# Two layers of a hybrid decoder trunk: the forget gates' chain goes first in both layers, and the final norm's steps stand in another order

## The chip, the cores and the metric

The kernel runs on one core of one Trainium2 chip. The core has a matrix engine (TensorE, PE in the profile; its weight loads are PEld), three engines for elementwise work (VectorE is DVE, ScalarE is ACT, GpSimd is POOL) and SyncE (SP), which here issues nearly all DMA transfers. Each engine works through its own list of instructions in order; semaphores hold an instruction until what it needs is there. TensorE writes to PSUM, of which the kernel uses eight banks. The metric is the device time of one execution in microseconds.

## The reference: what is computed

528 positions (16 learned meta tokens and 512 real ones) of width 1024 pass through two layers. Each layer is

```
xn   = rmsnorm(h) ; proj = xn @ w_in        # q,k,v of 8 fox heads, 8 gate columns, q,k,v,g of 4 retention heads
logf = log_sigmoid(gate columns + bias) ; c = cumsum(logf over positions)
fox  = softmax(q.k/8 + c[t] - c[s], causal) @ v           # per head
ret  = silu(g) * groupnorm(decayed linear attention)      # per head
h    = h + concat(fox, ret) @ w_out
h    = h + (silu(hn @ w_gate) * (hn @ w_up)) @ w_down     # hn = rmsnorm(h)
```

and after both layers `rmsnorm(h)` without the meta tokens is returned. Everything is float32.

## The kernel before, in words

Activations lie transposed: the 1024 features of `h` are eight tiles of 128 partitions, the positions run along the free axis. A float32 product is made of three faster ones: each operand is split into a rounded part and a rest (`hi`, `lo`; `split`, L130 to L132, and `convert`), and `hi*hi`, `hi*lo` and `lo*hi` add up in one PSUM bank. ScalarE makes `hi` (whi, xh, ah, sqh), VectorE or, for some weights, GpSimd makes `lo`.

The order of the work. TensorE's list is written out by hand: `layer` builds a plan of steps, and `merge` and `spread` place attention steps between the dense products. The lists of the other engines are made by a planner at build time. It replays the program with its own estimates of times, and gives each engine, whenever it is free, the ready instruction that stands first in the program; instructions under `tc.high_priority()` come ahead of those that don't. An instruction under `pin` is fixed behind the one that was written before it on its engine. The planner also orders SyncE's transfers, and on the chip a transfer whose buffer isn't free holds up all that stand behind it on SyncE.

Weights come as blocks of 512 KB (raw, L147) into three buffers. A buffer is free again when `whi` and `wlo` have been made from it; those lie in a ring of two, so that a conversion waits in turn until TensorE is done with an older block.

The forget gates (`forget_gates`, `forget_sums`). TensorE multiplies the eight gate columns (L368). ScalarE copies the part of the product on partitions 32 to 39 (L374), VectorE adds it to the rest (L375), for two halves of the positions. Then: times the norm's R (L382), absolute value, exponential and logarithm on ScalarE (L383 to L385), the minimum with 0 (L386), a subtraction (L387), and a running sum along the positions (L388). The sums go to a piece of DRAM, `cdr` (L390), and come back per head as `bc`, one row on all partitions (L486, two buffers). The scores of the first head (L497) are PSUM products; VectorE masks them (L503) and combines them with `bc` (L504), and only this frees their bank. PSUM banks `psa` are handed out in turn, four of them, so a later transpose of values (L407) may wait until such a bank is read. In layer 0 all steps up to the logarithm have precedence, in layer 1 none. Around them VectorE also makes q and k from their products (L420 and L427, L433 and L441), ropes (cr and sr, L1258) and value parts (L447).

The end. In the last layer the last round of the down projection is done in two column blocks: A (272 positions) and B (240). Eight products each; after each one VectorE adds it to `h` (`add_part`, L1093). Block A's norm is computed while TensorE is at block B: the steps `after_0` to `after_7` are written between B's products, one behind each. `square_b` and `scale_b` are ScalarE's square of a block of `h` and its product with the norm's weights, `sum_b` (L1131) adds a square to `acc`, `sums` (L1159) adds over partitions on TensorE with a matrix of ones, `root` (L1147) is ScalarE's reciprocal root, `newton` (L1151 to L1155) are three VectorE steps that refine it, and `out_a` and `out_b` multiply two output tiles by the root (L1135) and send them to DRAM (L1138). B's sum of squares is made from five parts: `acc` of squares 0 to 4, split into `hi` and `lo` (L1209, L1210), and squares 5, 6 and 7 as they are. All B steps on VectorE and ScalarE are pinned; the one `out_a` on GpSimd and the transfers aren't.

Of the kernel before, what the change touches and what calls it, by code (L numbers as in the profile page):

```python
# [10 lines left out]
F32 = mybir.dt.float32  # L11
F32R = mybir.dt.float32r
AF = mybir.ActivationFunctionType
ALU = mybir.AluOpType
# [5 lines left out]
T = SEQ + META  # L20
DEPTH = 2
FH = 8
# [17 lines left out]
def hybrid_kernel(ctx, tc, x_t, w_in, w_fl, w_out, w_gate, w_up, w_down, vecs, b_fg, rope, decay, mask, ident, out_t):  # L40
    nc = tc.nc
# [15 lines left out]
    bfg = const.tile([FH, DEPTH], F32, name="bfg")  # L57
# [190 lines left out]
    def psum_a():  # L248
        return psa.tile([128, 512], F32, name="psa", tag="psa")
# [5 lines left out]
    def tt(name, dt=F32):  # L255
        tag, bufs = tags[name]
        return tmp.tile([128, T], dt, name=name, tag=tag, bufs=bufs)
# [38 lines left out]
    def pin(f, pinned=True):  # L296
        if pinned:
            tc.keep_in_program_order(f)
# [48 lines left out]
    def load_gates(l, st):  # L347
        st["wfr"] = wp.tile([128, NK, FH], F32, name="wfr", tag="wfr", bufs=1)
        nc.sync.dma_start(st["wfr"], w_fl[l])
# [6 lines left out]
    def forget_gates(l, st):  # L356
        if l:
            load_gates(l, st)
            gate_weights(l, st)
        else:  # L360
            for t, src in ((bfg, b_fg), (msk, mask), (idt, ident)):
                nc.sync.dma_start(t, src)
        wf = st["wf"]
        psf = [psum_a() for _ in FULL]
        for i in range(2 * NK):
            k, part = i // 2, i % 2
            for ps, (c0, c1) in zip(psf, FULL):
                nc.tensor.matmul(ps[:, 0:c1 - c0], wf[:, k, :], st["x"][k][part][:, c0:c1],  # L368
                                 start=(i == 0), stop=(i == 2 * NK - 1))
        z = tt("z")[0:FH]  # L370
        z2 = tt("z2")[0:FH]
        for ps, (c0, c1) in zip(psf, FULL):
            with ExitStack() if l else tc.high_priority():
                nc.scalar.copy(z2[:, c0:c1], ps[32:32 + FH, 0:c1 - c0])  # L374
                nc.vector.tensor_add(z[:, c0:c1], ps[0:FH, 0:c1 - c0], z2[:, c0:c1])  # L375
        st["z"] = z

    def forget_sums(l, st):
        z = st["z"]
        z2 = tt("z2")[0:FH]  # L380
        with ExitStack() if l else tc.high_priority():
            nc.vector.scalar_tensor_tensor(z, z, RSC, st["R"][0:FH, :], ALU.mult, ALU.mult)  # L382
            nc.scalar.activation(z2, z, AF.Abs, bias=bfg[:, l:l + 1])  # L383
            nc.scalar.activation(z2, z2, AF.Exp, scale=-1.0)
            nc.scalar.activation(z2, z2, AF.Ln, bias=onec[0:FH])  # L385
        nc.vector.tensor_scalar(z, z, bfg[:, l:l + 1], 0.0, ALU.add, ALU.min)  # L386
        nc.vector.tensor_sub(z, z2, z)  # L387
        nc.vector.tensor_tensor_scan(z2, z, z, 0.0, ALU.add, ALU.max)  # L388
        st["cdr"] = tc.dram_tile([FH, T], F32, name=f"cdr{l}")
        nc.sync.dma_start(st["cdr"], z2)  # L390

    LOGS = "natural_log_exp_and_others"
    ROOTS = "abs_reciprocal_sqrt_and_small"
# [419 lines left out]
    def ffn(l, st, real, last):  # L813
# [269 lines left out]
        else:  # L1083
# [4 lines left out]
            na, nb = PA[1] - PA[0], PB[1] - PB[0]  # L1088
            fin = {}
# [24 lines left out]
            def scale_b(*ms):  # L1114
                for m in ms:
                    pin(nc.scalar.activation(fin["yb"][:, m], h[m][:, cb], AF.Copy, scale=gf[:, m:m + 1]))

            def square_b(m):
                if m == 0:
                    t = fft("S", F32, (128, 6, w), 2)  # L1120
                    fin["one"] = [t[:, i, 0:nb] for i in range(3)]
                    fin["acc"], fin["rb"], fin["tb"] = (t[:, i, 0:nb] for i in range(3, 6))
                    d = fin["acc"]
                elif m < NK - 3:
                    fin["sq", m] = d = tt("sq")[:, 0:nb]
                else:
                    d = fin["one"][m - NK + 3]
                pin(nc.scalar.activation(d, h[m][:, cb], AF.Square))

            def sum_b(m):  # L1130
                pin(nc.vector.tensor_add(fin["acc"], fin["acc"], fin["sq", m]))  # L1131
# [8 lines left out]
            def out_a(eng, k):  # L1140
                out(eng, fin["ya"][k // HB][:, k % HB:k % HB + 2], fin["ra"], k, *PA)

            def out_b(eng, k):
                out(eng, fin["yb"][:, k:k + 2], fin["rb"], k, *PB)
# [4 lines left out]
            def newton(i, r, v, a):  # L1149
                if i == 0:  # L1150
                    pin(nc.vector.tensor_mul(a, r, r))  # L1151
                elif i == 1:
                    pin(nc.vector.scalar_tensor_tensor(a, v, D * EPS, a, ALU.add, ALU.mult))
                else:
                    pin(nc.vector.scalar_tensor_tensor(r, a, 3.0 * D, r, ALU.subtract, ALU.mult))  # L1155

            def sums(v, parts):
                for i, t in enumerate(parts):
                    nc.tensor.matmul(v, ones if t.dtype == F32R else ones.bitcast(F32), t, start=(i == 0), stop=(i == len(parts) - 1))  # L1159
# [23 lines left out]
            def after_2():  # L1183
                fin["va"] = psum_a()[:, 0:na]
                sums(fin["va"], fin["a"][0:2])
                fin["ra"], fin["ta"] = (fft("e", F32, (128, T), 2)[:, 0:na] for _ in range(2))
                root(fin["ra"], fin["va"])
                sum_b(1)
                square_b(2)

            def after_3():
                for i in range(3):
                    newton(i, fin["ra"], fin["va"], fin["ta"])
                sum_b(2)
                square_b(3)
                scale_b(0)
                out_a(nc.gpsimd, 0)

            def after_4():
                sum_b(3)  # L1200
                square_b(4)
                scale_b(1)
                out_a(nc.vector, 2)

            def after_5():
                sum_b(4)
                square_b(5)
                hi, lo = tt("sqh", F32R)[:, 0:nb], tt("sql", F32R)[:, 0:nb]
                pin(nc.scalar.copy(hi, fin["acc"]))  # L1209
                pin(nc.vector.tensor_sub(lo, fin["acc"], hi.bitcast(F32)))  # L1210
                fin["b"] = hi, lo
                scale_b(2)

            def after_6():
# [2 lines left out]
            def after_7():  # L1217
                hi, lo = fin["b"]
                square_b(7)
                v = psum_a()[:, 0:nb]  # L1220
                sums(v, (hi, lo, fin["one"][0], fin["one"][1], fin["one"][2]))
                out_a(nc.vector, 4)
                out_a(nc.vector, 6)
                scale_b(3, 4)
                root(fin["rb"], v)
                scale_b(5, 6, 7)
                for i in range(3):
                    newton(i, fin["rb"], v, fin["tb"])
                for k in range(0, NK, 2):
                    out_b(nc.vector, k)  # L1230
# [193 lines left out]
```

## Time and profile before

| | us |
|---|---|
| median of 3 runs (lowest to highest) | 1272.61 (1271.99 to 1272.77) |
| the profiled execution | 1272.43 |
| its span, first to last instruction | 1270.6 |
| TensorE busy in it | 1253.3 (99%) |
| VectorE, ScalarE, GpSimd busy | 998.6, 687.3, 266.9 |
| granted TensorE clock, mean | 0.999 |

A timeline row has its start in microseconds from the beginning of the span, the busy time, the engine and line, the operation, the tile written and the tiles read with their shapes, and how many instructions the row joins. A bracket gives the idle time of the engine in front of it and whose work ended that. Layer 0 takes the span's first half, layer 1 starts near 644, and the last round of the down projection near 1242. Matmuls are pipelined and their ends are modelled, so the rows of TensorE overlap.

### The profile page before, as it was taken

To read this page: it belongs to the slowest core of one execution; us is meant where nothing else is said; L and a number is where in the kernel's file an instruction comes from. 1 tells how busy PE (TensorE), PEld (TensorE's weight loads), DVE (VectorE), ACT (ScalarE), POOL (GpSimd) and SP (SyncE) were. 2 spreads that over 40 slices of the span, in tenths; PEclk is the share of its full clock that TensorE was granted. 3 is DMA by queue.
4 is the path that set the end of the run, shared out by engine and by line. 5 is a ranking of instruction groups with operands and counts; after the bars stand their busy time and mean duration, and the time that the engine had idled before them with its cause. 6 is when DMAs were issued, how large, how long until landed. Compare 5 with 4: busy or idle time off the path is not lost.

```text
span 1270.6 us, 23600 instructions
## 1 busy us (share of the span) xinstructions
PE 1253.3 (99%) x9263; PEld 1195.1 (94%) x9263; DVE 998.6 (79%) x1852; ACT 687.3 (54%) x1246; POOL 266.9 (21%) x527
## 2 busy tenths in 40 slices
PE   9999999999999999999999999999999999999997
PEld 8899999999999999999998989998789999999996
DVE  8878756779888888887786877567899888888866
ACT  7666545676444444444465665456764444444444
POOL 3455545410000000000025546454100000000000
PEclk9999999999999999999999999999999999999999
DMA  6322222123233333332323232222233333333321
GB/s 217 95 71 89 87 81 83 60 68 129 92 96 100 100 100 100 100 100 84 107 70 117 61 101 83 78 90 67 100 96 121 100 100 100 100 100 100 102 81 67
DMA packets 45680, 120.57 MB, mean 95 GB/s; under 512 B 5360, under 2 KB 12272, under 8 KB 45568
## 3 DMA queue, kind: packets, MB, share of 16 engines
q1 hardware_dynamic: 45136, 118.77, 29.7%
q8 instruction: 73, 1.20, 0.4%
q14 instruction: 39, 0.32, 0.1%
q10 hardware_dynamic: 432, 0.29, 0.1%
HBM read 116.91 MB, written 2.13 MB: 94 GB/s over the span
## 4 chain that ended last, share of the span: by engine, by line
PE 93%; DVE 2%; ACT 2%; DMA 2%; issue 0%; SPq 0%; DVEq 0%; ACTq 0%
PE psd L206 29%; PE psa L900 19%; PE psd L1035 14%; PE psd L900 13%; PE psa L206 5%; PE psa L1035 4%; PE psa L407 2%; PE psa L582 2%; PE psa L497 2%; PE psa L749 1%; PE psa L719 1%; DMA bc<-cdr 1%; DMA h<-x_t 0%; DMA cdr<-z 0%; PE psa L279 0%
## 5 line engine op out<-in xcount | busy, mean ns | idle before, releaser
L183 POOL TENSOR_TENSOR wlo<-raw,whi 128x128 fp32r<-128x128 f32 x504 | 261.4, 554 | 270.0 <-ACT whi L180 250.0
L206 PE MATMUL psd<-xh,whi 128*128 128x264 f32 (+1 forms) x792 | 195.4, 314 | 0.2 <-ACT whi L180 0.2
L206 PE MATMUL psd<-xl,whi 128*128 128x264 f32 (+1 forms) x792 | 186.0, 302 | 0.5 <-DVE xl L309 0.4
L206 PE MATMUL psd<-xh,wlo 128*128 128x264 f32 (+1 forms) x792 | 186.4, 303 | 0.0
L206 PEld LDWEIGHTS psd<-xh,whi 128*128 128x128 f32 x792 | 128.0, 189 | 5.2 <-ACT whi L180 0.9
L206 PEld LDWEIGHTS psd<-xh,wlo 128*128 128x128 f32 x792 | 126.8, 188 | 6.3 <-DVE wlo L183 0.6
L206 PEld LDWEIGHTS psd<-xl,whi 128*128 128x128 f32 x792 | 127.4, 188 | 5.0 <-DVE xl L309 1.2
L180 ACT CAST whi<-raw 128x512 fp32r<-128x512 f32 (+1 forms) x168 | 98.4, 613 | 49.3 <-PE psd L206 36.4
L888 ACT CAST whi<-raw 128x1024 fp32r<-128x1024 f32 (+2 forms) x62 | 54.8, 885 | 51.3 <-PE psd L900 39.9
L888 ACT CAST fwhi<-raw 128x1024 fp32r<-128x1024 f32 (+2 forms) x62 | 55.6, 897 | 47.5 <-PE psd L900 40.0
L1135 POOL TENSOR_TENSOR th<-th,e 128x544 f32<-128x544 f32 x1 | 1.4, 1370 | 359.1 <-DVE e L1155 359.1
L85 POOL MEMSET kl<- 64x528 f32 x2 | 1.1, 534 | 345.4 <-PE psa L900 345.4
L889 DVE TENSOR_TENSOR wlo<-raw,whi 128x1024 fp32r<-128x1024 f32 (+2 forms) x62 | 62.9, 1015 | 12.8 <-ACT whi L888 12.7
L889 DVE TENSOR_TENSOR fwlo<-raw,fwhi 128x1024 fp32r<-128x1024 f32 (+2 forms) x62 | 64.0, 1032 | 10.5 <-ACT fwhi L888 10.1
L900 PE MATMUL psa<-th,whi 128*128 128x264 f32 (+1 forms) x232 | 65.4, 282 | 0.0
L900 PE MATMUL psa<-th,wlo 128*128 128x264 f32 (+1 forms) x232 | 65.4, 282 | 0.0
L900 PE MATMUL psa<-tl,whi 128*128 128x264 f32 (+1 forms) x232 | 65.3, 282 | 0.0
L900 PE MATMUL psa<-th,fwhi 128*128 128x264 f32 (+1 forms) x224 | 63.4, 283 | 0.0
L900 PE MATMUL psa<-tl,fwhi 128*128 128x264 f32 (+1 forms) x224 | 63.3, 283 | 0.0
L900 PE MATMUL psa<-th,fwlo 128*128 128x264 f32 (+1 forms) x224 | 63.3, 282 | 0.0
L517 ACT ACTIVATE pd<-pd,nmax 128x144 f32<-128x144 f32 (+1 forms) x64 | 36.9, 576 | 43.8 <-DVE nmax L504 31.8
L966 ACT COPY e<-psa 128x264 f32<-128x264 f32 (+1 forms) x114 | 42.9, 376 | 28.4 <-PE psa L900 24.1
(343 smaller groups left out, 4053.5 us busy)
## 6 DMA issues: line engine op xcount, KB each, us to landing
raw<-w_in SPq DMA_DIRECT2D x54, 512.0 KB, 3.4
raw<-w_gate SPq DMA_DIRECT2D x44, 512.0 KB, 3.8
fraw<-w_up SPq DMA_DIRECT2D x38, 512.0 KB, 3.5
raw<-w_down SPq DMA_DIRECT2D x64, 256.0 KB, 2.8
raw<-w_out SPq DMA_DIRECT2D x16, 512.0 KB, 3.4
raw<-w_down SPq DMA_DIRECT2D x32, 192.0 KB, 2.5
bc<-cdr SPq DMA_DIRECT2D x16, 264.0 KB, 3.5
raw<-w_up SPq DMA_DIRECT2D x6, 512.0 KB, 3.5
```

The lines of the kernel that those rows point to most:

```text
L180: pin(nc.scalar.copy(hi, job["raw"][:, c0:c1]), pinned)
L183: pin(sub(lo[:, i:i + wide], job["raw"][:, c0 + i:c0 + i + wide], hi[:, i:i + wide].bitcast(F32)), pinned)
L206: nc.tensor.matmul(ps[1][b][:, 0:c1 - c0], w[:, wk, :], x[:, c0:c1], start=(k == 0 and i == 0), stop=(k == n - 1 and i == 2))
L407: nc.tensor.transpose(ps[:, 128 * j:128 * j + 128], src[:, o:o + 128], idt)
L497: nc.tensor.matmul(sc[0:nq, 0:c1 - c0], st["q"][s][:, q0:q0 + nq], kk[:, c0:c1], start=(i == 0), stop=(i == 1))
L517: nc.scalar.activation(pr, pr, AF.Exp, bias=nmax[0:nq], scale=-1.0, accum_out=rsum)
L582: nc.tensor.matmul(po[:, c0:SEQ], v[:, j, :], pp[:, j, META + c0:T], start=(j == 0 and i == 0), stop=(j == 4 and i == 1))
L888: nc.scalar.copy(hi, src)
L889: nc.vector.tensor_sub(lo, src, hi.bitcast(F32))
L900: nc.tensor.matmul(bank()[:, 0:b.shape[-1]], a[:, o + k, :], b, start=(fresh and k == 0 and i == 0), stop=(k == n - 1 and i == 2), skip_gr ...
L966: nc.scalar.copy(self.t["e"][:, i], self.t["x"][:, 0:w])
L1035: nc.tensor.matmul(v[:, 0:c1 - c0], a[:, s * n + k, :], b[:, c0:c1], start=(k == 0 and i == 0), stop=(k == n - 1 and i == 2))
```

## The change

Forget gates: in both layers the whole chain, from the copies of the product to the transfer of the sums to DRAM, is under `tc.high_priority()`; before, this held in layer 0 up to the logarithm. The minimum with 0 is written right behind the absolute value.

The end: the three `newton` steps of block A stand behind `root` (`after_2`) instead of behind product 3's addition; `sum_b(2)` moves from `after_3` to `after_4` and `sum_b(3)` from `after_4` to `after_5`; output pair 0 goes from GpSimd to VectorE and one step later, pair 2 to `after_7`; the `lo` part of B's sum is made behind the last addition instead of behind `hi`, and TensorE adds square 5 between `hi` and `lo`; pair 6 is written behind the root's and the scales' lines.

```diff
-            with ExitStack() if l else tc.high_priority():
+            with tc.high_priority():
                 nc.scalar.copy(z2[:, c0:c1], ps[32:32 + FH, 0:c1 - c0])
                 nc.vector.tensor_add(z[:, c0:c1], ps[0:FH, 0:c1 - c0], z2[:, c0:c1])
...
-        with ExitStack() if l else tc.high_priority():
+        with tc.high_priority():
             nc.vector.scalar_tensor_tensor(z, z, RSC, st["R"][0:FH, :], ALU.mult, ALU.mult)
             nc.scalar.activation(z2, z, AF.Abs, bias=bfg[:, l:l + 1])
+            nc.vector.tensor_scalar(z, z, bfg[:, l:l + 1], 0.0, ALU.add, ALU.min)
             nc.scalar.activation(z2, z2, AF.Exp, scale=-1.0)
             nc.scalar.activation(z2, z2, AF.Ln, bias=onec[0:FH])
-        nc.vector.tensor_scalar(z, z, bfg[:, l:l + 1], 0.0, ALU.add, ALU.min)
-        nc.vector.tensor_sub(z, z2, z)
-        nc.vector.tensor_tensor_scan(z2, z, z, 0.0, ALU.add, ALU.max)
-        st["cdr"] = tc.dram_tile([FH, T], F32, name=f"cdr{l}")
-        nc.sync.dma_start(st["cdr"], z2)
+            nc.vector.tensor_sub(z, z2, z)
+            nc.vector.tensor_tensor_scan(z2, z, z, 0.0, ALU.add, ALU.max)
+            st["cdr"] = tc.dram_tile([FH, T], F32, name=f"cdr{l}")
+            nc.sync.dma_start(st["cdr"], z2)
...
                 square_b(2)
-
-            def after_3():
                 for i in range(3):
                     newton(i, fin["ra"], fin["va"], fin["ta"])
-                sum_b(2)
+
+            def after_3():
                 square_b(3)
                 scale_b(0)
-                out_a(nc.gpsimd, 0)
 
             def after_4():
+                sum_b(2)
+                square_b(4)
+                out_a(nc.vector, 0)
+                scale_b(1)
+
+            def after_5():
                 sum_b(3)
-                square_b(4)
-                scale_b(1)
-                out_a(nc.vector, 2)
-
-            def after_5():
                 sum_b(4)
                 square_b(5)
-                hi, lo = tt("sqh", F32R)[:, 0:nb], tt("sql", F32R)[:, 0:nb]
-                pin(nc.scalar.copy(hi, fin["acc"]))
-                pin(nc.vector.tensor_sub(lo, fin["acc"], hi.bitcast(F32)))
-                fin["b"] = hi, lo
+                fin["b"] = tt("sqh", F32R)[:, 0:nb], tt("sql", F32R)[:, 0:nb]
+                pin(nc.scalar.copy(fin["b"][0], fin["acc"]))
                 scale_b(2)
...
             def after_7():
                 hi, lo = fin["b"]
                 square_b(7)
+                pin(nc.vector.tensor_sub(lo, fin["acc"], hi.bitcast(F32)))
                 v = psum_a()[:, 0:nb]
-                sums(v, (hi, lo, fin["one"][0], fin["one"][1], fin["one"][2]))
+                sums(v, (hi, fin["one"][0], lo, fin["one"][1], fin["one"][2]))
+                out_a(nc.vector, 2)
                 out_a(nc.vector, 4)
-                out_a(nc.vector, 6)
                 scale_b(3, 4)
                 root(fin["rb"], v)
                 scale_b(5, 6, 7)
+                out_a(nc.vector, 6)
```

## The prediction

> **What bounds the kernel now.** I read the page first, then the TensorE rows of the timeline wherever the list of TensorE's waits names one, then each stall backwards through the other engines' timelines. The page's first row, and the five TensorE rows with an idle time that the change can reach (the bracket is the idle time and who ended it):
>
> ```profile
> PE 1253.3 (99%) x9263; PEld 1195.1 (94%) x9263; DVE 998.6 (79%) x1852; ACT 687.3 (54%) x1246; POOL 266.9 (21%) x527
> 35.15 0.18 PE L497 MATMUL psa<-kl,qs 128*16 128x16 f32 x1 [0.92 <-DVE kl L441]
> 39.86 0.40 PE L497 MATMUL psa<-kh,qs 128*128 128x272 f32 x1 [0.72 <-DVE nmax L504]
> 677.38 0.66 PE L407 MATMUL psa<-idt,vd 128*128 128x128 f32 x4 [0.48 <-DVE nmax L504]
> 679.84 0.30 PE L407 MATMUL psa<-idt,vd 128*128 128x128 f32 x1 [1.80 <-DVE vv L473]
> 1260.70 0.38 PE L1159 MATMUL psa<-sqh,ones 128*128 128x240 f32 x1 [1.26 <-ACT sqh L1209]
> ```
>
> TensorE is busy for 1253.3 of 1270.6 us and the change takes no product away, so it can win only in the 17.3 us between: 1.64 in layer 0 (two stalls), 2.28 in layer 1 (two stalls), and what follows the last product. VectorE and ScalarE matter only where TensorE waits for them.
>
> **Layer 1's gates.** ScalarE, VectorE, SyncE and VectorE again, each in order of time; the scan's result goes to DRAM (cdr) and comes back as rows (bc) that the first scores need:
>
> ```profile
> 654.54 0.64 ACT L374 COPY z<-psa 8x264 f32<-8x264 f32 x2 [2.15 <-PE psa L368]
> 654.70 0.69 DVE L420 SCALAR_TENSOR_TENSOR tq<-psd,R 128x512 f32<-128x512 f32 x1
> 655.31 1.02 DVE L1258 SCALAR_TENSOR_TENSOR cr<-cr,R 128x528 f32<-128x528 f32 x1
> 656.25 0.41 DVE L375 TENSOR_TENSOR z<-psa,z 8x264 f32<-8x264 f32 x1
> 656.69 1.40 DVE L427 TENSOR_TENSOR qs<-tq,qs 64x512 fp32r<-64x512 f32 x2
> 658.13 0.42 DVE L375 TENSOR_TENSOR z<-psa,z 8x264 f32<-8x264 f32 x1
> 658.48 0.68 DVE L1258 SCALAR_TENSOR_TENSOR sr<-sr,R 128x528 f32<-128x528 f32 x1
> 659.09 0.69 DVE L382 SCALAR_TENSOR_TENSOR z<-z,R 8x528 f32<-8x528 f32 x1
> 662.03 0.70 DVE L387 TENSOR_TENSOR z<-z,z 8x528 f32<-8x528 f32 x1 [0.34 <-ACT z L385]
> 662.76 1.40 DVE L388 TENSOR_TENSOR_SCAN z<-z 8x528 f32<-8x528 f32 x1
> 668.09 0.33 SPq L147 DMA_DIRECT2D raw<-w_in  x1
> 668.47 0.32 SPq L390 DMA_DIRECT2D cdr<-z  x1
> 671.68 0.81 SPq L486 DMA_DIRECT2D bc<-cdr  x2
> 672.66 6.54 SPq L147 DMA_DIRECT2D raw<-w_in  x2
> 671.53 0.30 DVE L503 TENSOR_TENSOR psa<-psa,msk 128x128 f32<-128x128 f32 x1 [4.59 <-PE psa L497]
> 675.70 0.31 DVE L504 CUSTOM_DVE_ANT_0 pd<-psa,bc 128x144 f32<-128x144 f32 x1 [3.88 <-DMA bc<-cdr]
> ```
>
> The gates' chain is interrupted three times: cr (655.31 to 656.25, 0.94), the two qs (656.69 to 658.13, 1.44) and sr (658.48 to 659.09, 0.61). With precedence these 2.99 us stand behind it; ScalarE's copies are done by 655.18, so nothing else holds the additions. I leave tq in front: it is ready as soon as R is, perhaps before the copies. If the additions pass it too, 0.61 more. From L382 to the scan VectorE's order is already as short as ScalarE's three functions allow, so the scan ends at 662.76 + 1.40 - 2.99 = 661.17 instead of 664.16.
>
> The result then lay ready 4.31 us, because SyncE stood at a weight load (668.09) that waited for a buffer. Two bounds. If the planner, which now has the result some 3 us sooner, puts cdr ahead of that load, cdr goes out at 661.2, 7.3 us sooner; if behind it, no sooner than the buffer is free: nothing, or as much as ScalarE, freed sooner from the gates, converts that buffer sooner. I take cdr ahead, since the distance it was late by (4.31) is the weight buffer's and the chain gains 2.99 on a load whose conversion is tied to TensorE's progress. The bc loads may still be caught behind the weight load; even then they go at 668.4 instead of 671.68, 3.3 us sooner, because the round trip through cdr has happened in the meantime. VectorE waited 3.88 us for bc and both TensorE stalls, 0.48 and 1.80, follow from its late start, so 3.3 us covers the 2.28. **Term: -2.28, bounds 0 and -2.28.**
>
> What is moved back: cr and sr have no reader before the first rotation, the q parts none before the first scores at about 671, and VectorE then stands still for 4.59 us in front of the scores; the 2.99 us fit there. Without that cover they would cost at most themselves. cdr passes one weight load on SyncE, whose own issue takes 0.33.
>
> **Layer 0's gates.** Here the sums and everything up to the logarithm already had precedence; new are the minimum, the subtraction, the scan and the transfer.
>
> ```profile
> 31.70 0.68 DVE L433 SCALAR_TENSOR_TENSOR tq<-psd,R 128x528 f32<-128x528 f32 x1
> 32.31 0.69 DVE L387 TENSOR_TENSOR z<-z,z 8x528 f32<-8x528 f32 x1
> 33.27 1.24 DVE L388 TENSOR_TENSOR_SCAN z<-z 8x528 f32<-8x528 f32 x1
> 34.43 1.40 DVE L441 TENSOR_TENSOR kl<-tq,kh 64x528 fp32r<-64x528 f32 x2
> 32.41 2.60 ACT L440 CAST kh<-tq 64x528 fp32r<-64x528 f32 x4 [0.82 <-DVE tq L433]
> ```
>
> Lower bound: only the one piece of the value part (L447) that stands between subtraction and scan steps back. Subtraction to scan is 0.96 here and 0.73 in layer 1, so 0.23. Upper bound: the subtraction also passes tq, scan at 31.70 + 0.73 = 32.43, 0.84 sooner. But then k's tq starts at about 33.6, four kh copies of 0.65 follow it, and kl is there about 0.45 later than now: the stall at 35.15 grows by 0.45, and takes that from the 0.72 at 39.86. TensorE then reaches 39.86 - 0.72 + 0.45 = 39.6, a gain of 0.3. A loss would need kl more than 0.72 later, which the whole of subtraction and scan doesn't do. **Term: -0.25, bounds 0 and -0.84.**
>
> **The end.** VectorE from the first sum on, then GpSimd, ScalarE, TensorE's last five products as the chain of what ended last has them, and its last sums:
>
> ```profile
> 1254.51 0.40 DVE L1131 TENSOR_TENSOR S<-S,sq 128x240 f32<-128x240 f32 x1
> 1255.44 0.41 DVE L1093 TENSOR_TENSOR h<-psa,h 128x240 f32<-128x240 f32 x1 [0.54 <-PE psa L900]
> 1255.77 0.43 DVE L1151 TENSOR_TENSOR e<-e 128x272 f32<-128x272 f32 x1
> 1257.07 0.40 DVE L1131 TENSOR_TENSOR S<-S,sq 128x240 f32<-128x240 f32 x1
> 1257.70 1.25 DVE L1131 TENSOR_TENSOR S<-S,sq 128x240 f32<-128x240 f32 x1
> 1258.88 0.71 DVE L1135 TENSOR_TENSOR th<-th,e 128x544 f32<-128x544 f32 x1
> 1259.51 0.39 DVE L1093 TENSOR_TENSOR h<-psa,h 128x240 f32<-128x240 f32 x1
> 1260.68 0.41 DVE L1210 TENSOR_TENSOR sql<-S,sqh 128x240 fp32r<-128x240 f32 x1 [0.46 <-ACT sqh L1209]
> 1263.50 0.41 DVE L1151 TENSOR_TENSOR S<-S 128x240 f32<-128x240 f32 x1 [0.51 <-ACT S L1147]
> 1257.32 1.37 POOL L1135 TENSOR_TENSOR th<-th,e 128x544 f32<-128x544 f32 x1 [359.12 <-DVE e L1155]
> 1254.43 0.49 ACT L1147 ACTIVATE e<-psa,epsc 128x272 f32<-128x272 f32 x1
> 1254.40 5.06 PE psa L900 x45
> 1261.36 1.61 PE L1159 MATMUL psa<-S,ones 128*128 128x240 f32 x6
> ```
>
> The addition of product 5 starts at 1259.51, though a product takes 1.01 us (5.06 by five) and this one, two before the last, was done near 1259.46 - 2.02 = 1257.4. ScalarE's square 5 and hi copy queue behind it, TensorE waits 1.26 us for hi, lo comes at 1260.68, and the sums end at 1261.36 + 1.61 = 1262.97. So VectorE sets the end.
>
> The new order, by start-to-start times from these rows: independent additions 0.33 (1255.44 to 1255.77), the Newton triple 1.30 (1255.77 to 1257.07), a scaled pair 0.63 (1258.88 to 1259.51), a sum behind a sum 0.46 (1.30 less one independent step, by two). The first root ends at 1254.92, just as sum 1 does, so Newton starts at 1254.95. Addition 3: 1256.25; addition 4: 1256.58; sum 2: 1256.91; output pair 0, now VectorE's: 1257.24; addition 5: 1257.87; sum 3: 1258.20; sum 4: 1258.66, done 1259.06; addition 6: 1258.99. Addition 7 is held by its product, done at 1259.46: 1259.50. ScalarE's hi copy is ready then, lo runs from 1259.83 to 1260.24, and TensorE has hi and the first square behind it. From lo to the end remain lo (0.22) and four of the six records (1.07): 1261.5, instead of 1262.97. The three output pairs on VectorE reach 1259.83 + 0.33 + 1.89 = 1262.05; the second root ends about there too. Newton at 1262.08 instead of 1263.50. **Term: -1.4.** The slack in front of addition 7 is only 0.2 us, so everything slower by more than that returns one for one: bounds -0.6 and -1.6. The transfers of pairs 2 and 4 now leave near 1261, not earlier than before for pair 2; the last transfer, not these, ends the kernel.
>
> The addition at 1257.70 took 1.25 us under GpSimd's product, its neighbours 0.40; I count 0.40. The Trainium skill (GPSIMD Engine Reference, Specifications) says that GpSimd shares its SBUF interfaces with VectorE and collides with instructions that read two SBUF inputs, as this addition does: by that rule the trace agrees and the 0.85 comes back. Were the 1.25 the addition's own, lo would be 0.85 less 0.2 later and the sum 1269.2.
>
> **Sum.** 2.28 + 0.25 + 1.4 = 3.93 off the profiled execution's 1272.43 us (span 1270.6 and 1.83 around it) gives 1268.5. The runs' median, 1272.61, is 0.18 above that execution: I say 1268.6.
>
> **Rivals.** *Layer 1's stall stays*, because cdr keeps its place behind the weight load and that buffer is freed when it is now: 1272.43 - 1.65 = 1270.8. For it: the planner's order is decided by its own reckoning, not by 668.09; against it: 2.99 us are much for one place. *The end gives its gain back*: Newton now stands in front of addition 3 and waits for a root that ended 0.03 us before it; a root 1.4 us later, or the fourth output pair in front of the second Newton (0.63) with the slack of 0.2 used up, leaves 1272.43 - 2.53 = 1269.9. *The change does not do what it says*: the planner's order moves little, and the end is bound by transfers: 1272.4. *Slower*: the rows behind the weight loads. bc is not given precedence, and if the planner puts both bc behind the pair of weight loads of 672.66, whose second goes at 672.66 + 6.54 - 0.33 = 678.87, they leave 7.5 us later than now and TensorE stands for it: 1272.43 + 7.5 - 1.65 = 1278.3. It decides from 4.2 us of delay on (1.65 gained elsewhere, 2.55 to be measured). For it: just such a queue costs 4.31 us now. Against: bc's source is ready sooner, not later.
>
> **How the numbers follow.** Forecast 0.56 (own range 1267.2 to 1270.0), stall stays 0.17, end given back 0.12, nothing 0.07, slower 0.08. Below 1266.9 nothing is left to win (2.28 + 0.84 + 1.6 = 4.72, and measurement); above 1271.6 lie "nothing" and "slower", and little of the rest. A difference of 0.2%, 2.5 us, is what a measurement here can tell from none: faster by that takes nearly all of the forecast and over half of "given back" and a little of "stays", 0.65; slower 0.08; the rest 0.27.
>
> **What would show it.** Layer 1: L375 twice in succession near 655, the scan ending near 661, cdr in front of a weight load, no TensorE idle at the first value transposes. Layer 0: scan near 33, kl's stall no larger than 1.4. The end: no GpSimd row, no sum longer than 0.5, hi's matmul right behind the last product, Newton near 1.4 us sooner against the last product. Wrong would be: cdr still behind the load, a new idle time at the k parts, or VectorE still busy with output pairs when the second root is done.

## The result and the profile after

The changed kernel takes 1268.75 us (median of 8 runs, 1268.37 to 1269.62), the kernel before beside it 1272.69 (8 runs, 1271.92 to 1274.86): a ratio of 0.9969 with a 95% interval of 0.9958 to 0.998. That is 3.94 us less. The profiled execution's span went from 1270.6 to 1266.7.

The page's first row after. TensorE's busy time is nearly what it was (1253.3 before), so most of the gain comes out of its idle time:

```profile
PE 1252.7 (99%) x9263; PEld 1195.0 (94%) x9263; DVE 998.3 (79%) x1853; ACT 686.9 (54%) x1246; POOL 265.0 (21%) x526
```

**Layer 1's gates after**: VectorE's timeline, then SyncE's, then the second group of value transposes on TensorE, which had the idle times before.

```profile
655.71 1.01 DVE L1257 SCALAR_TENSOR_TENSOR cr<-cr,R 128x528 f32<-128x528 f32 x1
656.64 0.75 DVE L375 TENSOR_TENSOR z<-psa,z 8x264 f32<-8x264 f32 x2
657.42 0.69 DVE L427 TENSOR_TENSOR qs<-tq,qs 64x512 fp32r<-64x512 f32 x1
658.14 0.70 DVE L382 SCALAR_TENSOR_TENSOR z<-z,R 8x528 f32<-8x528 f32 x1
661.82 1.40 DVE L388 TENSOR_TENSOR_SCAN z<-z 8x528 f32<-8x528 f32 x1
672.27 0.31 DVE L504 CUSTOM_DVE_ANT_0 pd<-psa,bc 128x144 f32<-128x144 f32 x1
...
663.25 0.29 SPq L390 DMA_DIRECT2D cdr<-z  x1
666.96 0.34 SPq L147 DMA_DIRECT2D raw<-w_in  x1
667.35 0.91 SPq L486 DMA_DIRECT2D bc<-cdr  x2
...
677.15 0.71 PE L407 MATMUL psa<-idt,vd 128*128 128x128 f32 x5
```

The scan ends at 663.22 instead of 664.16. The larger step is SyncE's: cdr goes out 0.03 us after the scan, ahead of the weight load (666.96) behind which it stood before. The loads of bc leave at 667.35 instead of 671.68, though they still stand behind that weight load. VectorE's first L504 has no bracket (3.88 before), and all five transposes run as one group without an idle time (0.48 and 1.80 before).

**Layer 0 after**: VectorE around the scan, then TensorE's two stalls.

```profile
32.97 0.69 DVE L387 TENSOR_TENSOR z<-z,z 8x528 f32<-8x528 f32 x1
33.58 0.41 DVE L447 SCALAR_TENSOR_TENSOR vd<-psa,R 128x264 f32<-128x264 f32 x1
33.92 1.24 DVE L388 TENSOR_TENSOR_SCAN z<-z 8x528 f32<-8x528 f32 x1
...
35.81 0.18 PE L497 MATMUL psa<-kl,qs 128*16 128x16 f32 x1 [0.90 <-DVE kl L441]
40.27 0.40 PE L497 MATMUL psa<-kh,qs 128*128 128x272 f32 x1 [0.49 <-DVE nmax L504]
```

The order is that of before: subtraction, a value piece, scan, with the same steps from row to row (0.96 from subtraction to scan before, 0.95 now). Both stalls are there. The rows up to kl's stall are 0.66 us later than before, because this execution began later (0.68 at layer 0's first transposed product; of that more at the end).

**The end after**: VectorE, then ScalarE's hi copy, hi's sum on TensorE, and the last five products as the chain of what ended last has them. There is no GpSimd row.

```profile
1254.52 0.40 DVE L1131 TENSOR_TENSOR S<-S,sq 128x240 f32<-128x240 f32 x1
1254.84 0.72 DVE L1135 TENSOR_TENSOR th<-th,e 128x544 f32<-128x544 f32 x1
1255.47 0.40 DVE L1093 TENSOR_TENSOR h<-psa,h 128x240 f32<-128x240 f32 x1
1255.79 0.91 DVE L1131 TENSOR_TENSOR S<-S,sq 128x240 f32<-128x240 f32 x2
1256.61 0.89 DVE L1093 TENSOR_TENSOR h<-psa,h 128x240 f32<-128x240 f32 x2
1257.42 0.40 DVE L1217 TENSOR_TENSOR sql<-S,sqh 128x240 fp32r<-128x240 f32 x1
1257.74 1.99 DVE L1135 TENSOR_TENSOR th<-th,e 128x544 f32<-128x544 f32 x3
1259.65 0.40 DVE L1151 TENSOR_TENSOR S<-S 128x240 f32<-128x240 f32 x1
...
1256.73 0.39 ACT L1208 CAST sqh<-S 128x240 fp32r<-128x240 f32 x1 [0.42 <-DVE S L1131]
...
1257.17 0.38 PE L1159 MATMUL psa<-sqh,ones 128*128 128x240 f32 x1
...
1252.02 5.06 PE psa L900 x45
```

The last product is done at 1252.02 + 5.06 = 1257.08 (1259.46 before). hi's sum follows it 0.09 us later with no idle time (1.26 before). Newton starts 2.57 us behind the last product instead of 1263.50 - 1259.46 = 4.04, so 1.47 sooner. From the last product to the end of the span it was 1270.6 - 1259.46 = 11.14 us and is now 9.62.

**Where the time went.** Two points in the trace cut the span into three parts: layer 0's first product of probabilities and values (L574; the first row below is the kernel before, the second the changed one) and the end of the last product.

```profile
56.79 0.17 PE L574 MATMUL psa<-pth,vv 128*128 128x16 f32 x1
```

```profile
57.20 0.17 PE L574 MATMUL psa<-pth,vv 128*128 128x16 f32 x1
```

| us | before | after | difference |
|---|---|---|---|
| start of the span to L574 | 56.79 | 57.20 | +0.41 |
| L574 to the end of the last product (layer 1's gates lie in it) | 1202.67 | 1199.88 | -2.79 |
| end of the last product to the end of the span | 11.14 | 9.62 | -1.52 |
| span | 1270.6 | 1266.7 | -3.9 |

### The profile page after: what moved, and what is told of

Its sections match the earlier page's. It is cut to its first block, busy times and chain, and to the rows that moved or that the text cites. A ratio compares the mean times of both kernels' runs of the same rounds, so it can differ in the third digit from the quotient of the medians.

```text
span 1266.7 us, 23601 instructions
## 1 busy us (share of the span) xinstructions
PE 1252.7 (99%) x9263; PEld 1195.0 (94%) x9263; DVE 998.3 (79%) x1853; ACT 686.9 (54%) x1246; POOL 265.0 (21%) x526
## 4 chain that ended last, share of the span: by engine, by line
PE 94%; DVE 2%; ACT 2%; DMA 1%; issue 0%; DVEq 0%; ACTq 0%; SPq 0%
PE psd L206 30%; PE psa L900 19%; PE psd L1035 14%; PE psd L900 13%; PE psa L206 5%; PE psa L1035 4%; PE psa L407 2%; PE psa L582 2%; PE psa L497 2%; PE psa L749 1%; PE psa L719 1%; DMA h<-x_t 0%; ACT whi L180 0%; PE psa L279 0%; ACT sq L325 0%
## 5 line engine op out<-in xcount | busy, mean ns | idle before, releaser
L888 ACT CAST fwhi<-S 128x1024 fp32r<-128x1024 f32 x20 | 21.0, 1049 | 68.6 <-PE psa L900 66.5
```

Source lines behind the costliest of these rows:

```text
L888: nc.scalar.copy(hi, src)
```

## The experiments

Each kernel was timed in five rounds against the kernel before; the first four shared one set of its runs, the next four another, the last three a third. Between traces with the same order in layer 1 and at the end, the last two of the three parts above repeat within about 0.1 us, much better than whole times, so the text goes by them.

**The gates' part alone and the end's part alone.** The first kernel is the kernel before with the diff's lines in `forget_gates` and `forget_sums` only, the second with those from `after_2` to `after_7` only. The lines that the first has and the second has not, shortened:

```diff
-            with ExitStack() if l else tc.high_priority():
+            with tc.high_priority():
...
+            nc.vector.tensor_scalar(z, z, bfg[:, l:l + 1], 0.0, ALU.add, ALU.min)
...
+            nc.sync.dma_start(st["cdr"], z2)
```

> The kernel before with the gates' part of the change alone; the end as before. Theory (the gates' gain is layer 1's two TensorE stalls, 0.48 and 1.80 us, gone because the row loads bc leave sooner): 2.3 to 2.7 us less than before, 1270.0 to 1270.4, and 11.1 us from the last product's end to the span's end, as before. Rival (the end makes the whole gain): no difference from before.

> The kernel before with the end's part of the change alone; the gates as before. Theory: 1.4 to 1.5 us less than before, 1271.1 to 1271.3; layer 1's two stalls stay at 2.3 us; 9.6 us from the last product's end to the span's end instead of 11.1. Rival (the two parts are not additive, the end gains only with TensorE earlier): less than 0.5 us.

Gates only: 1270.25 us (11 runs, 1269.39 to 1271.35), a ratio of 0.9981 (0.9973 to 0.999). End only: 1271.19 (11 runs, 1270.49 to 1272.91), 0.9989 (0.998 to 0.9998). The kernel before beside them took 1272.65, so the parts are worth 2.40 and 1.46, together 3.86 of the 3.94: they add up and hardly touch each other. In the traces, gates only leaves 11.09 us behind the last product and brings 1199.81 from L574 to it; end only leaves 9.60, with 1202.35. The stalls of layer 1 are gone in the first and stay in the second, whose rows are:

```profile
677.21 0.66 PE L407 MATMUL psa<-idt,vd 128*128 128x128 f32 x4 [0.17 <-DVE nmax L504]
679.67 0.30 PE L407 MATMUL psa<-idt,vd 128*128 128x128 f32 x1 [1.80 <-DVE vv L473]
```

**Is it the chain or the place on the queue?** The kernel before with one line changed: in layer 1 ScalarE issues cdr instead of SyncE. The chain of the gates has no precedence here.

```diff
-        nc.sync.dma_start(st["cdr"], z2)
+        (nc.scalar if l else nc.sync).dma_start(st["cdr"], z2)
```

> The kernel before, no precedence anywhere new; only layer 1's transfer of the sums, cdr, is issued by ScalarE instead of SyncE, so that it does not stand behind the weight load. Theory (the place on SyncE's queue makes the stall, the length of the gates' chain does not): cdr leaves right behind the scan, near 664.3 instead of 668.5, bc near 668.5 instead of 671.7, the stalls of 0.48 and 1.80 are gone, 2.3 to 2.7 us less than before. Rival (the chain itself is too late): bc leaves under 2 us sooner and at least 0.6 us of the stalls stays.

1270.85 us (11 runs, 1270.14 to 1272.09), a ratio of 0.9983 (0.9974 to 0.9991). VectorE's scan, ScalarE's issue, SyncE, VectorE's first L504 and TensorE's transposes:

```profile
663.86 1.40 DVE L388 TENSOR_TENSOR_SCAN z<-z 8x528 f32<-8x528 f32 x1
...
665.29 0.53 ACTq L390 DMA_DIRECT2D cdr<-z  x1
...
669.64 0.90 SPq L486 DMA_DIRECT2D bc<-cdr  x2
...
673.84 0.31 DVE L504 CUSTOM_DVE_ANT_0 pd<-psa,bc 128x144 f32<-128x144 f32 x1 [0.91 <-DMA bc<-cdr]
...
677.85 0.71 PE L407 MATMUL psa<-idt,vd 128*128 128x128 f32 x5
```

The chain is as long as before (scan done at 665.26, in an execution that runs about a microsecond later), and yet both stalls are gone, with 0.91 us of VectorE's wait left over. From L574 to the last product it takes 1199.99 us, against 1202.67 before and 1199.88 in the changed kernel. So in layer 1 the place of cdr on SyncE's queue is nearly all of the gain; the sooner end of the scan adds 0.1 us in the changed kernel's trace and not quite 0.2 in that of the gates alone. The medians of this kernel and of the gates alone stand further apart (1.80 and 2.40 below the kernel before) than these stretches (2.68 and 2.86), within what the executions' starts scatter by.

**Layer 0: sums ahead of q's part.** The changed kernel left layer 0's order alone. Here the plan's step that makes the sums is written ahead of the step that finishes q:

```diff
-... + gates + stats + [lambda: ly["wait"].pop(0)()] + sums + [lambda: ly["wait"].pop(0)()]
+... + gates + stats + sums + [lambda: ly["wait"].pop(0)(), lambda: ly["wait"].pop(0)()]
```

> The changed kernel, in layer 0 the gates' sums written ahead of the q part, so that they come ahead of q's product reading on VectorE and of the q copies on ScalarE. Theory (layer 0's two stalls, 0.90 at the k part and 0.49 at the row load, hang on the gates' chain): the chain ends 0.7 to 1.3 us sooner, the two stalls shrink by 0.7 to 1.3, 1267.4 to 1268.1. Rival (q and k parts moved back take the place): the stall at the first scores grows by as much as the other shrinks, 1268.7 or more.

1268.57 us (5 runs, 1267.35 to 1269.4), a ratio of 0.9965 (0.9953 to 0.9978): not to be told from the changed kernel, so the expected gain was missed. kl's stall is gone, but the planner put q's differences between subtraction and scan, the scan ended hardly sooner, and the stall that waits for the rows stayed:

```profile
32.03 0.70 DVE L387 TENSOR_TENSOR z<-z,z 8x528 f32<-8x528 f32 x1
32.76 0.70 DVE L427 TENSOR_TENSOR qs<-tq,qs 64x528 fp32r<-64x528 f32 x1
...
39.94 0.39 PE L497 MATMUL psa<-kh,qs 128*128 128x272 f32 x1 [0.48 <-DVE nmax L504]
```

Precedence given to one chain did nothing here: between two of its steps the planner still gave VectorE another step.

**The end's single steps.** Three kernels, each the changed kernel with one thing as it was before: output pair 0 on GpSimd; the Newton triple behind addition 3; lo right behind hi, with TensorE adding hi, lo, squares.

```diff
-                out_a(nc.vector, 0)
+                out_a(nc.gpsimd, 0)
```

```diff
                 square_b(2)
-                for i in range(3):
-                    newton(i, fin["ra"], fin["va"], fin["ta"])
 
             def after_3():
+                for i in range(3):
+                    newton(i, fin["ra"], fin["va"], fin["ta"])
```

```diff
                 pin(nc.scalar.copy(fin["b"][0], fin["acc"]))
+                pin(nc.vector.tensor_sub(fin["b"][1], fin["acc"], fin["b"][0].bitcast(F32)))
...
-                pin(nc.vector.tensor_sub(lo, fin["acc"], hi.bitcast(F32)))
...
-                sums(v, (hi, fin["one"][0], lo, fin["one"][1], fin["one"][2]))
+                sums(v, (hi, lo, fin["one"][0], fin["one"][1], fin["one"][2]))
```

> The changed kernel, with the first output pair (th<-th,e at the end) multiplied on GpSimd again instead of VectorE. In the changed kernel the last product's end is followed by 9.62 us to the end of the span. Theory (GpSimd's product slows a two-input addition of VectorE that runs beside it from 0.40 to about 1.2 us): a row psa/S L1131 or L1093 of over 1 us stands beside the GpSimd row, but VectorE is freed of 0.63 us of its own product, so the two nearly cancel: the additions behind are at most 0.2 us later, the end 9.5 to 9.8 us behind the last product, the time within 0.2 us of the changed kernel's. Rival (the 1.25 of the kernel before was that addition's own): no row over 0.5 us beside GpSimd's product, VectorE up to 0.6 us ahead in front of the seventh addition, the end 9.4 to 9.6. What tells them apart is the length of the row, not the time.

> The changed kernel, with the first Newton triple behind addition 3 instead of in front of it (the order of the kernel before). Theory of the prediction (VectorE sets the end, with a slack of only 0.2 us in front of the last addition): additions 4 to 6 start where they do now or up to 0.47 us later, since a dependent triple costs the same in either place but addition 3 no longer fills a gap; lo and the last sums are 0.1 to 0.3 us later, the end 9.7 to 9.9 us behind the last product instead of 9.62. Rival (the place of the triple doesn't matter, the gain of the end comes from the fewer instructions in front of lo and from GpSimd's absence): 9.6.

> The changed kernel, with lo (L1217) made right behind ScalarE's hi copy, ahead of the last two additions, and TensorE's last sums in the order hi, lo, squares, as in the kernel before. Theory (VectorE is in order, and lo waits for ScalarE's copy of hi, which holds up the two additions behind it): VectorE idles 0.4 to 0.5 us in front of lo, the last addition is 0.3 to 0.5 us later, and with it the last square, the last sums and the Newton triple: 9.9 to 10.1 us from the last product to the end instead of 9.62. Rival (the place of lo hardly matters since the last addition has slack): 9.6.

| | median us (runs, range) | ratio to before (95%) | Newton behind the start of the last product's last record |
|---|---|---|---|
| changed kernel | 1268.75 (8; 1268.37 to 1269.62) | 0.9969 (0.9958 to 0.998) | 2.86 |
| pair 0 on GpSimd | 1268.73 (5; 1267.91 to 1269.46) | 0.9967 (0.9955 to 0.998) | 2.93 |
| Newton behind addition 3 | 1269.09 (6; 1268.48 to 1269.63) | 0.997 (0.9959 to 0.9982) | 3.18 |
| lo right behind hi | 1269.04 (6; 1268.27 to 1269.74) | 0.9969 (0.9958 to 0.9981) | 3.23 |
| kernel before | 1272.69 (8; 1271.92 to 1274.86) | | 4.34 |

The first and the last row are those of the result; beside the three kernels the kernel before took 1273.02 (11 runs, 1271.77 to 1273.4). The medians can't tell differences of some tenths; the last column can (a second trace of the changed kernel has 2.86 again). From the last product's end to the span's end the three take about 9.7, 10.0 and 10.0 us, so the second is a little above what was expected. GpSimd's product and VectorE's addition of square 2 in the first of the three:

```profile
1254.96 1.38 POOL L1135 TENSOR_TENSOR th<-th,e 128x544 f32<-128x544 f32 x1 [358.34 <-PE psa L900]
...
1255.33 1.26 DVE L1131 TENSOR_TENSOR S<-S,sq 128x240 f32<-128x240 f32 x1
```

The addition beside GpSimd's product takes 1.26 us, the same one in the changed kernel 0.40 (1254.52 above): it is the product on the other engine that stretches it, by 0.86. Here and in the kernel before, the addition ends 0.25 and 0.26 us behind GpSimd's product, so what it loses depends on where in that product it starts. Moving the product to VectorE costs 0.63 there and saves 0.86. Of the balance, 0.17 falls into VectorE's wait in front of addition 7 (additions 6 and 7 take 0.89 us in the changed kernel and 0.72 here), and the exchange itself is worth only 0.07 at Newton. The other two are steps of the order, and each costs what the engine in order has to wait. In the second kernel VectorE stands idle for 0.54 us in front of addition 3, where the changed kernel runs Newton. In the third kernel VectorE stands at lo for ScalarE's copy, and additions 6 and 7 behind it:

```profile
1257.45 0.41 DVE L1209 TENSOR_TENSOR sql<-S,sqh 128x240 fp32r<-128x240 f32 x1 [0.46 <-ACT sqh L1208]
```

Undone one at a time they cost 0.07, 0.32 and 0.37 us, together 0.76 of the 1.48. The first two push addition 5 back by 0.24 and 0.49 us and lose the 0.17 each time, so single steps add up to less than the whole. The rest wasn't taken apart: pair 2 behind the last addition and the sums one product later weren't tried alone.

**Layer 0's chain really first.** With the sums ahead in the plan, the copies and differences of the first head's q are also kept by the planner behind logarithm and scan (`last` holds the two), and cr and sr behind the scan:

```diff
+                with tc.issue_after(ly["last"][0]) if first else ExitStack(), tc.issue_after(ly["last"][1]) if first else ExitStack():
                     nc.scalar.copy(sv(t, real, a0, a1), sv(tq, real, a0, a1))
                     nc.vector.tensor_sub(sv(t, real, b0, b1), sv(tq, real, a0, a1), sv(t, real, a0, a1).bitcast(F32))
...
+                with tc.issue_after(ly["last"][1]) if l == 0 else ExitStack():
                     nc.vector.scalar_tensor_tensor(t, t, RSC, ly["R"], ALU.mult, ALU.mult)
```

> The changed kernel, with layer 0's gate chain really given the way free that the prediction had at its upper bound: there the copies and differences of q's parts stand behind the logarithm and the scan, and the first rotation's factors (cr, sr) behind the scan. In the changed kernel the order of layer 0 is that of the kernel before on every engine, and its two stalls (0.90 at the k part, 0.49 at the scores) are as before. Theory (the 0.49 is the wait for the scan's result as rows): the scan ends 1.0 to 1.5 us sooner against the first product, the stall at the scores disappears, the time 0.4 to 0.6 us below the changed kernel's. Rival (q's parts are now the late ones): a new idle time of TensorE in front of the first scores of as much or more, the time equal or up to 1 us longer.

1267.34 us (5 runs, 1266.7 to 1267.72), a ratio of 0.9957 (0.9943 to 0.997). The scan, cdr, bc, and TensorE's stall at kl, which is the only one left of the two:

```profile
31.29 1.23 DVE L388 TENSOR_TENSOR_SCAN z<-z 8x528 f32<-8x528 f32 x1
...
32.55 0.30 SPq L391 DMA_DIRECT2D cdr<-z  x1
34.02 0.80 SPq L488 DMA_DIRECT2D bc<-cdr  x2
...
34.77 0.18 PE L499 MATMUL psa<-kl,qs 128*16 128x16 f32 x1 [0.67 <-DVE kl L443]
```

Counted from layer 0's first transposed product, the scan starts 1.83 us sooner than in the changed kernel (31.29 - 22.76 against 33.92 - 23.56) and L574 comes 0.97 us sooner (32.67 against 33.64). That is more than the 0.4 to 0.6 expected, and more than the stall at the scores was.

**Side by side, and one step further.** The changed kernel, the kernel just shown, and that kernel with the two value pieces (L449) also behind the scan, all in the same rounds:

```diff
+                with tc.issue_after(ly["last"][1]) if first else ExitStack():
                     nc.vector.scalar_tensor_tensor(vt[:, c0:c1], t[:, 0:c1 - c0], RSC, ly["R"][:, c0:c1], ALU.mult, ALU.mult)
```

> The changed kernel itself, on the same chip and in the same rounds as the next two kernels, so that their difference of about 1 us can be read against it. Expected 3.9 us below the kernel before, as in its own result.

> The changed kernel with layer 0's gate chain ahead of q's parts and of the first rotation's factors, once more, beside the changed kernel. In the trace its first value product came 0.97 us sooner, counted from layer 0's first transposed product. Theory (that is the whole gain, the rest of the 1.4 us between the two medians was the executions' start): 0.8 to 1.2 us below the changed kernel. Rival (the distance of the medians is the gain): 1.4 us below.

> As the kernel beside it, with layer 0's two value pieces (L449) also behind the scan and, in the order that results, behind the k parts. In the kernel beside it the second piece stands between subtraction and scan, and TensorE still waits 0.67 us for kl. Theory (what stands in front of kl on VectorE sets that wait): scan 0.3 us and kl 0.6 to 0.7 us sooner, the wait gone or below 0.1, the time 0.5 to 0.7 us less. Rival (TensorE or the rows of the gates become the next bound): kl's wait shrinks and a wait for the rows (nmax) or for the value pieces takes its place, the time equal within 0.3.

| | median us (runs, range) | ratio to before (95%) | first transposed product to L574 |
|---|---|---|---|
| changed kernel | 1268.67 (6; 1268.46 to 1269.89) | 0.9969 (0.9957 to 0.998) | 33.60 |
| layer 0's chain first | 1267.48 (5; 1266.84 to 1268.38) | 0.996 (0.9947 to 0.9972) | 33.25 |
| and value pieces behind | 1268.68 (6; 1267.39 to 1269) | 0.9967 (0.9955 to 0.998) | 33.12 |

The kernel before took 1272.81 beside them (11 runs), so the changed kernel is 4.14 us below it, where 3.9 were expected. The chain first is 1.19 us below the changed kernel, and the longest of its times is shorter than the changed kernel's shortest. It has the lowest median found, here and in its own rounds. But this time its trace shows only 0.35 us of it in layer 0, where the transfer of cdr took longer: from cdr's issue to bc's it was 1.47 us in the trace above, lies between 1.47 and 1.50 in all the others, and is 2.46 here, and VectorE waits for bc again.

```profile
32.76 0.30 SPq L391 DMA_DIRECT2D cdr<-z  x1
35.22 0.81 SPq L488 DMA_DIRECT2D bc<-cdr  x2
```

So neither 0.97 nor 1.19 can be given as the gain of this order; it is 0.35 to 0.97 in the two traces, and the remainder of the medians' distance lies in the executions' starts or isn't explained. The measure itself scatters: in the nine traces that have the changed kernel's order in layer 0 the distance from the first transposed product to L574 is 33.32 to 33.91 us, so 33.25 is hardly outside. The third kernel bore its theory out only in the small: kl's wait went from 0.65 to 0.42 and not to nothing, and a wait for the value transposes grew from 0.21 to 0.46 in exchange, as the rival had it.

```profile
34.75 0.18 PE L499 MATMUL psa<-kl,qs 128*16 128x16 f32 x1 [0.42 <-DVE kl L443]
41.29 0.74 PE L408 MATMUL psa<-idt,vd 128*128 128x128 f32 x5 [0.46 <-DVE vv L475]
```

Why its median is 1.2 us above its neighbour's is open: its profiled execution, 1267.39 us, is one of its two shortest, so the trace doesn't show what the longer ones have. Its six times lie in two groups, 1267.39 and 1267.52 and then 1268.53 to 1269, which is about as far as the starts of two executions of one kernel can lie apart (last section); that the longer four started so isn't shown.

## Why the prediction was right, and where it was not

**The time.** 1268.6 was said, 1268.75 came. The profiled execution, against which the sum was made, lost 3.9 us of span where 3.93 were said. The terms were not that exact: layer 1 gave 0.51 more than its term and the end 0.12 more, layer 0 gave nothing that can be told from zero, and the later start took 0.41. That these cancelled to 0.1 us is luck. (The working's own sum from the median, 1272.61 less 3.93, is 1268.68; and its formula for a sum behind a sum gives 0.485 and not 0.46. Neither changes anything.) Two of the signs it named didn't come: the scan in layer 1 ended at 663.22 and not near 661, and layer 0's started at 33.92 and not near 33.

**Layer 1 (said -2.28, measured -2.79): the mechanism was right, two of its steps were not, and the size was off.** cdr ahead of the weight load, bc still behind one, both stalls gone: this came as written. But the scan was to end 2.99 us sooner, at 661.17, and that failed. R is 0.40 us later in the trace after (L289 at 654.11 against 653.71), and against it the scan ends 0.94 + 0.40 = 1.34 sooner. Precedence passed one qs (0.72) and sr (0.61). It didn't pass cr (0.94) and the first qs (0.72): cr was issued at 655.71, although ScalarE's copies were done by 655.6 and L375 could have gone: the planner's times, not the chip's, decide what is ready. That cost nothing: the experiment with cdr on ScalarE's queue shows that no sooner end of the scan was needed. The prediction made too much of the chain and tied the planner's choice to it; the choice itself was the cause.

The size: the two brackets, 0.48 and 1.80, were added up as what could be won. Three kernels without them are 2.68 (cdr on ScalarE), 2.79 (changed) and 2.86 (gates only) shorter between L574 and the last product. The missing part stands in the same rows. These are, before and after, the last score product ahead of the transposes and the first dense product behind them:

```profile
676.56 0.34 PE L497 MATMUL psa<-kl,qs 128*128 128x400 f32 x1
679.90 0.48 PE L206 MATMUL psd<-xh,whi 128*128 128x512 f32 x1
```

```profile
676.97 0.34 PE L497 MATMUL psa<-kl,qs 128*128 128x400 f32 x1
677.61 0.48 PE L206 MATMUL psd<-xh,whi 128*128 128x512 f32 x1
```

From start to start that is 3.34 us before and 0.64 after, which is 2.70 of the 2.79. A bracket begins at the modelled end of the row in front. But rows that don't wait start ahead of that end: after, the transposes start at 677.15, 0.18 us behind the start of a row of 0.34. So the two stalls cost 0.64 and 2.06 us, 0.16 and 0.26 more than their brackets say. This is the term that was mis-sized; it should have been taken from starts. The remaining 0.09 is not accounted for.

**Layer 0 (said -0.25, found nothing that can be told from zero).** The step that failed is the lower bound, by which the piece of the value part between subtraction and scan steps back. It didn't; the order on VectorE and ScalarE is the same. L574 comes 0.27 us sooner against the first transposed product (33.64 instead of 33.91), but two traces with the same gates, gates only (33.34) and the changed kernel beside others (33.60), differ by as much, and the trace with cdr on ScalarE's queue, whose layer 0 has the gates as before, has 33.32. The upper bound of 0.84, scan sooner by passing tq (of which the working itself let 0.3 reach TensorE), was drawn too low for what is possible there: with q's part out of the way the scan went 1.83 us sooner, and L574 0.35 to 0.97.

**The end (said -1.4, measured -1.5): right step by step.** Counted from the last product's end, the working had addition 5 at -1.59, lo at 0.37 and Newton at 2.62; they stand at -1.61, 0.34 and 2.57. The third output pair and the root were said to end at about the same time: 1259.73 and 1259.57. The additions take 0.40 without GpSimd's product, as counted, and the experiment that puts it back shows 1.26 beside it; the rule of the Trainium skill (GPSIMD Engine Reference, Specifications) that GpSimd and VectorE share the interface agrees with that row. One thing came out differently: the chain that ended last now runs through the three output pairs on VectorE and no longer through TensorE's sums and the root.

```profile
1257.82 1.90 DVE th L1135 x3
1259.73 0.33 DVE S L1151
```

The slack of 0.2 us in front of addition 7 was about right (0.17): Newton late and lo early, which use it up, cost 0.32 and 0.37 where 0.1 to 0.3 and 0.3 to 0.5 were expected.

**The rivals.** *Layer 1's stall stays* fell with cdr's place. *The end gives its gain back*: its second case, output pairs in front of the second Newton, is real (the chain above, one of the prediction's own signs of being wrong) but worth 0.16 us at most, since the root is done only that much before the pairs. *Slower*: both bc still stand behind a weight load, as that rival had it, but behind one that leaves at 666.96; the two that wait longer (670.61 to 677.03) come behind bc.

## What to carry to other kernels

When a result lies ready and TensorE waits for it, look first at what stands ahead of its transfer on the issuing queue: here one transfer behind a weight load that had no free buffer cost 2.7 us, and moving it to another engine's queue won nearly as much as giving its whole chain of arithmetic precedence. A precedence mark didn't pass every step that it was meant to pass, so compare the order of instructions before and after, engine by engine, before counting a gain. At the end of a kernel, keep the instructions between the last product and the last store in the order in which their inputs arrive; the two steps that were put out of that order cost 0.3 to 0.4 us each. Times of single executions, which scatter by over a microsecond, don't show that, while distances inside the trace do. And take what a stall of TensorE costs from the starts of the rows around it: here the brackets of 2.28 us stood for 2.70.

## What the hardware showed that was not expected

The same kernel starts its first products at two speeds. Two of TensorE's first dense products in the trace of the changed kernel, and then in the second trace of the same kernel:

```profile
5.92 0.41 PE L206 MATMUL psd<-xl,whi 128*128 128x264 f32 x2
6.16 0.40 PE L206 MATMUL psd<-xh,wlo 128*128 128x264 f32 x2
```

```profile
6.13 0.64 PE L206 MATMUL psd<-xl,whi 128*128 128x264 f32 x2
6.57 0.64 PE L206 MATMUL psd<-xh,wlo 128*128 128x264 f32 x2
```

A pair of products takes 0.24 us from start to start in the first and 0.44 in the second, until 10.97, though the granted clock is shown as 1.00 in both over that time. The first transposed product of layer 0 then stands at 23.56 and 24.73, and the spans, 1266.7 and 1267.8, differ by the same 1.1 to 1.2 us. The Trainium skill (TensorE: Matmul & The Clock Gate, What's actually happening) says that the array runs at half its clock until a window of steady work is over and that the number of slow products varies from run to run because that window is free-running; the two rates, 1.8 apart, are near that. But the page lets the end of the slow rate vary by half a microsecond either way; here it was over by 5.56 in the first trace and lasted until 10.97 in the second, with the same seven products (3.35 us, from 1.59) in front, so in these runs it varied by over 5 us. The thirteen traces here have none to twelve such pairs, and their first transposed product stands between 22.76 and 24.73. This isn't all of the scatter. The kernel before and the changed kernel's first trace are both without such pairs, and the later start in the first table (0.41 us at L574) begins with the first dense product, which waited 0.16 us for its weights before and began at 5.11, and 0.62 us after and began at 5.56. Nothing of the change lies ahead of that product, so the later start isn't counted against it.
